# First block of a two-block model: lo parts of 15 weight tiles by an adding DMA, second gate moved behind the last chunk sum, two output tables moved ahead of the recurrence

## Chip, cores and metric

The kernel runs on one core of a Trainium2 chip. The metric is the device time of one execution in microseconds; several executions are taken and the median is given.

## What is computed

The reference takes x of 512 tokens by 1024 channels through two blocks. Only the first is touched by the change. It is, cut to what matters:

```python
h = _rms_norm(x, pre_norm_g)
z_q, z_kv, z_kr, g_attn, u_ssm, g_ssm = split(h @ w_in)       # 256, 128, 64, 512, 512, 512
attn = _mla_attention(z_q, z_kv, z_kr, ...)                   # 4 heads, q and k with a rotary part
attn = _rms_norm(attn) * silu(g_attn)
ssm = _s5_bidirectional(u_ssm, ...)                           # 32 groups, 64 complex states, both directions
ssm = gelu(ssm); ssm = ssm * sigmoid(ssm @ w_glu + b_glu)
ssm = _rms_norm(ssm) * silu(g_ssm)
x = x + _rms_norm(concat([attn, ssm]) @ w_out)
```

The second block is two layers of sparse and forgetting attention, each with a feed-forward part.

## The kernel before

**Precision by splitting.** A product of float32 matrices is made of three matmuls (`mm3`, lines 172 to 176). Each operand is split into hi, its value rounded to the matmul's format, and lo, what is left: hi times hi, hi times lo and lo times hi are added up in PSUM. For weights this is done in `weights` (lines 146 to 167): SyncE loads a block of 512 KB into a staging tile `wst` (two buffers), ScalarE casts it to hi (`whi`, line 143), VectorE subtracts, staging minus hi, to lo (`wlo`, line 144). With `pool` set, GpSimd makes lo instead; the diff leaves that branch alone. There are four `whi` and four `wlo` buffers, so a block's split can start only when an earlier block's matmuls are done with theirs.

**The first block in order.** `block1` (lines 305 to 844) norms and transposes x into `xT`, and multiplies it by the weights of u. The state-space part runs by chunks: for each of eight slices of four groups, `f_slice` (lines 463 to 481) makes a table on VectorE (`table`, lines 450 to 458: a product into `tb`, a product into `ot`, and their sum), transposes it on TensorE (`ftr`), copies it out on ScalarE (`f`) and multiplies it by u (`vps`, line 478), which gives the chunk sums; ScalarE copies them into `st`. The recurrence over the chunk sums (`recur`, lines 503 to 518) is a chain of VectorE operations on `st`: 13 steps of four operations (lines 498 to 501) and 16 fix-up operations (lines 517 and 518).

Next in program order are the two gates (lines 610 to 617, each four outputs of 24 matmuls by `feat`), the z tiles (`z_tile`, lines 629 to 653: `tok`, a norm with a row sum on GpSimd, a transpose), the matmuls for V (line 666), for the rotary part of q (lines 668 to 686, four rounds of matmul, VectorE, ScalarE, transpose), and then a list of rounds (line 770) which interleaves three kinds of generators: `prep(s)` (lines 533 to 562: the output table of slice s, its store to `Ed` in DRAM, and the kernel matrix `kps` with its store to `Kd`), `y_slice(s)` (lines 566 to 600: reads both back, copies `st` into `X`, and multiplies) and `head(h)` (lines 704 to 767: one attention head). After them come the gated unit, the output projection and the norms.

**What sets the order.** The program order gives priorities alone. A scheduler of the framework places each engine's instructions by priority and by a simulated timeline, so an engine can run a later stage's instruction while an earlier one's inputs are missing; once placed, the order on an engine is fixed and each instruction waits for its inputs. `tc.issue_after(ins)` adds an edge: the instructions traced inside it on the engine of `ins` stand behind `ins` in that engine's order. Tiles of one tag share a few buffers: `tb` two (tag E), `ot` and the fix-ups' `fx` one (tag et).

Of the kernel before, what the change touches and what calls it, by code (L numbers as in the profile page):

```python
# [12 lines left out]
AF = mybir.ActivationFunctionType  # L13
OP = mybir.AluOpType
# [13 lines left out]
SL0 = 3  # L28
# [12 lines left out]
def rounds(items, heads=()):  # L41


    items, r = list(items), 0
    while items:
        now = [x for x in items if x[0] <= r]
        late = [x for x in now if x[1] in heads]
        done = []
        for x in [x for x in now if x[1] not in heads] + late[1:] + late[:1]:
            if next(x[1], done) is done:  # L50
                done.append(x)
        items = [x for x in items if x not in done]
        r += 1
# [10 lines left out]
class Net:  # L64
# [78 lines left out]
        self.nc.scalar.copy(hi, src)  # L143
        self.nc.vector.tensor_tensor(lo, src, hi.bitcast(F32), OP.subtract)  # L144

    def weights(self, blocks, cw=512, n=2, pool=False, into=None, stage=None):

        nc = self.nc
        hs, ls = [], []
        for i, b in enumerate(blocks):  # L150
            if stage is None:
                st = self.wpool.tile([128, n, 1024 // n], F32, tag="stage", bufs=2, name="wst")
                nc.sync.dma_start(st[:, :, :cw], b)
            else:
                st = stage[:, i]
            h, l = into or (self.wpool.tile([128, n, 1024 // n], F32R, tag=t, bufs=self.slots["w"], name=t)
                            for t in ("whi", "wlo"))
            if pool is True or pool and i in pool:
                nc.scalar.copy(h[:, :, :cw], st[:, :, :cw])
                for j in range(n):  # L160
                    self.lo(l[:, j, :cw], st[:, j, :cw], h[:, j, :cw])
            else:
                self.split(h[:, :, :cw], l[:, :, :cw], st[:, :, :cw])
            for j in range(n):
                hs.append(h[:, j, :cw])
                ls.append(l[:, j, :cw])
        return hs, ls
# [137 lines left out]
    def block1(self):  # L305

        nc, A, tc = self.nc, self.A, self.tc
        mm = nc.tensor.matmul
# [46 lines left out]
        def feat(wh, wl, m):  # L355
            p = self.ps("mm")
            ms = slice(m * 128, (m + 1) * 128)
            for k in range(8):
                self.mm3(self.tiled(p), wh[k][:, ms], wl[k][:, ms], xh[k], xl[k], k == 0, k == 7)
            return p  # L360
# [99 lines left out]

        st = self.act(shape=[128, G, 2, 8, 8], name="st", tag="C")

        def f_slice(s):
            gs = slice(s * 4, s * 4 + 4)
            ft = table(FP, FQ, br[:, gs], bi[:, gs], s)
            yield
            f = []
            for r in range(2):
                p = self.ps("sc" if s % 2 else "tr", "ftr")
                for gg in range(4):  # L470
                    nc.tensor.transpose(p[:, gg * 128:(gg + 1) * 128], ft[:, gg, r], self.ident)
                f.append(self.act(shape=[128, 4, 128], name="f", tag="PT"))
                nc.scalar.copy(f[r].rearrange("p g e -> p (g e)"), p)
            yield
            pv = self.ps("o", "vps").rearrange("p (g r c) -> p g r c", r=2, g=4)
            for r in range(2):
                for gg in range(4):
                    mm(pv[:, gg, r], f[r][:, gg], U[:, s * 4 + gg], start=True, stop=True)
            for ps_, o in ((slice(0, 64), 1), (slice(64, 128), -1)):
                nc.scalar.copy(st[ps_, gs].rearrange("p g r j s -> p (g r) j s"),  # L480
                               pv[ps_, :, :, ::o].rearrange("p g r (s j) -> p (g r) j s", j=8))
# [84 lines left out]
        def y_slice(s):  # L566
# [21 lines left out]
            if s % 2 == 1:  # L588
# [10 lines left out]
                nc.scalar.activation(q, q, AF.Tanh, scale=math.sqrt(2.0 / math.pi))  # L599
                nc.vector.scalar_tensor_tensor(sg[:, m], q, 1.0, p, OP.add, OP.mult)  # L600

        recur()


# [3 lines left out]
        nc.vector.tensor_scalar(gn[:, 1], gn[:, 1], 0.125, None, OP.mult)  # L608
        gate = [self.b8([128, 4, 512], F32, name="gate") for _ in range(2)]
        for i in range(2):  # L610
            wh, wl = self.weights([A["w1_in"][1 + i, j] for j in range(4)])
            for m in range(4):
                p = feat(wh, wl, m)
                th = self.act(name="th", tag="c")
                nc.scalar.activation(th, p, AF.Tanh, scale=0.5)
                nc.scalar.activation(gate[i][:, m], p, AF.Copy, scale=gn[:, i, m:m + 1])
                nc.vector.scalar_tensor_tensor(gate[i][:, m], th, 1.0, gate[i][:, m], OP.add, OP.mult)
# [6 lines left out]
        gqk = self.act(shape=[128, 384], name="gqk", tag="PT")  # L624
        nc.sync.dma_start(gqk, A["gqk"].to_broadcast([128, 384]))
        Z = [self.b8([128, 4, 512], name=n) for n in ("zh", "zl")]
        wh, wl = self.weights([A["w1_z"][i] for i in range(4)], 448)

        def z_tile(t):
            ts = slice(t * 128, (t + 1) * 128)  # L630
# [24 lines left out]
        rounds((t, z_tile(t)) for t in range(NT))  # L655


        wqr_h, wqr_l = self.weights([A["w_uq_r"]], 256)
        wk_h, wk_l = self.weights([A["w_ukv_t"]])
        wq_h, wq_l = self.weights([A["w_uq_n"]])  # L660
        V = [self.b8([128, 4, 512], name=n) for n in ("vh", "vl")]
        QR = self.b8([128, 4, 512], name="QR")
        for t in range(NT):
# [40 lines left out]
        def head(h):  # L704
# [52 lines left out]
            if SPLIT:  # L757
# [9 lines left out]
            nc.vector.tensor_tensor(gate[0][:, h], o, gate[0][:, h], OP.mult)  # L767

        sg = self.b8([128, 4, 512], F32, name="sg")
        rounds([(s, prep(s)) for s in range(8)] + [(SL0 + s, y_slice(s)) for s in range(8)]  # L770
               + [(HEAD0[h], head(h)) for h in range(4)])


# [753 lines left out]
```

## Time and profile before

| | us |
|---|---|
| median of 3 runs | 1667.33 |
| lowest, highest | 1665.48, 1668.69 |
| the profiled execution | 1673.57 |
| its span | 1671.8 |
| TensorE busy | 1593.8 (95%) |
| VectorE busy | 951.2 (57%) |
| ScalarE busy | 794.3 (48%) |
| GpSimd busy | 402.4 (24%) |

The profile is of one execution. PE is TensorE, DVE is VectorE, ACT is ScalarE, POOL is GpSimd, SPq is SyncE's queue of DMA issues. Matmuls overlap in their records, so a busy TensorE is not one at its peak; its granted clock, at full speed 1.00, tells how fast it could go. The first block takes the first 345 us or so of the span.

### The profile page before, as it was taken

To read this page: it belongs to the slowest core of one execution; us is meant where nothing else is said; L and a number is where in the kernel's file an instruction comes from. 1 tells how busy PE (TensorE), PEld (TensorE's weight loads), DVE (VectorE), ACT (ScalarE), POOL (GpSimd) and SP (SyncE) were. 2 spreads that over 40 slices of the span, in tenths; PEclk is the share of its full clock that TensorE was granted. 3 is DMA by queue.
4 is the path that set the end of the run, shared out by engine and by line. 5 is a ranking of instruction groups with operands and counts; after the bars stand their busy time and mean duration, and the time that the engine had idled before them with its cause. 6 is when DMAs were issued, how large, how long until landed. Compare 5 with 4: busy or idle time off the path is not lost.

```text
span 1671.8 us, 22665 instructions
## 1 busy us (share of the span) xinstructions
PE 1593.8 (95%) x8240; PEld 1345.8 (80%) x8240; DVE 951.2 (57%) x1863; ACT 794.3 (48%) x1548; POOL 402.4 (24%) x492
## 2 busy tenths in 40 slices
PE   7996899999999999999999999999989999999998
PEld 6884687787888888888888888788868888888886
DVE  8978767754687865323333365478875532333334
ACT  6634476543677845333232444368774433323242
POOL 2000013313455712001010140345580210101012
PEclk9998899999999999999999999899999999999999
DMA  5211452544322442332333334512234133333332
GB/s 172 75 56 38 129 146 76 184 119 156 92 59 53 119 134 75 96 95 89 101 101 101 114 109 128 161 45 58 64 102 126 51 101 101 101 101 101 101 96 81
DMA packets 71407, 167.44 MB, mean 100 GB/s; under 512 B 14464, under 2 KB 23168, under 8 KB 71296
## 3 DMA queue, kind: packets, MB, share of 16 engines
q1 hardware_dynamic: 70528, 165.21, 32.3%
q8 instruction: 65, 1.06, 0.3%
q10 hardware_dynamic: 768, 0.79, 0.2%
q14 instruction: 46, 0.38, 0.1%
HBM read 145.80 MB, written 10.98 MB: 94 GB/s over the span
## 4 chain that ended last, share of the span: by engine, by line
PE 70%; DVE 7%; ACT 3%; issue 3%; DMA 2%; POOL 1%; ACTq 1%; DVEq 0%; POOLq 0%; SPq 0%
PE mm L176 19%; PE mm L174 19%; PE mm L175 19%; PE cps L983 2%; PE ptr L943 2%; DVE sc L918 1%; DVE pt L144 1%; PE sc L917 1%; PE sc L914 1%; PE oacc L952 1%; PE oacc L953 1%; DVE wlo L144 1%; ACT ysq L206 1%; DMA ql<-ql 1%; ACT sc L921 1%
## 5 line engine op out<-in xcount | busy, mean ns | idle before, releaser
L144 DVE TENSOR_TENSOR wlo<-wst,whi 128x1024 fp32r<-128x1024 f32 (+3 forms) x209 | 253.7, 1218 | 248.8 <-ACT whi L143 245.1
L174 PE MATMUL mm<-xT,whi 128*128 128x512 f32 (+1 forms) x896 | 337.8, 380 | 4.3 <-ACT kf L1083 2.8
L143 ACT CAST whi<-wst 128x1024 fp32r<-128x1024 f32 (+3 forms) x209 | 215.3, 1034 | 256.6 <-PE mm L176 123.7
L175 PE MATMUL mm<-xT,whi 128*128 128x512 f32 (+1 forms) x896 | 335.5, 376 | 0.0
L176 PE MATMUL mm<-xT,wlo 128*128 128x512 f32 (+1 forms) x896 | 326.3, 376 | 0.9 <-DVE wlo L144 0.8
L1367 POOL TENSOR_TENSOR relu<-relu 128x512 f32<-128x512 f32 x64 | 67.1, 1048 | 539.6 <-ACT relu L1366 539.6
L176 PE MATMUL mm<-whi,hl 128*128 128x512 f32 x512 | 195.9, 389 | 0.0
L175 PE MATMUL mm<-wlo,hh 128*128 128x512 f32 x512 | 195.9, 389 | 0.0
L174 PEld LDWEIGHTS mm<-xT,whi 128*128 128x128 f32 x896 | 168.2, 189 | 33.4 <-ACT kf L1083 3.6
L176 PEld LDWEIGHTS mm<-xT,wlo 128*128 128x128 f32 x896 | 168.7, 189 | 32.1 <-DVE wlo L144 1.8
L175 PEld LDWEIGHTS mm<-xT,whi 128*128 128x128 f32 x896 | 168.9, 189 | 27.4
L174 PE MATMUL mm<-whi,hh 128*128 128x512 f32 x512 | 188.2, 389 | 0.0
L921 ACT ACTIVATE sc<-sc,mn 128x512 f32<-128x512 f32 x192 | 107.1, 559 | 32.9 <-DVE mn L918 25.2
L144 DVE TENSOR_TENSOR hl<-relu,hh 128x512 fp32r<-128x512 f32 x64 | 51.8, 810 | 119.4 <-ACT hh L143 117.1
L144 DVE TENSOR_TENSOR pt<-ptr,pt 128x256 fp32r<-128x256 f32 (+1 forms) x160 | 95.7, 605 | 40.0 <-ACT pt L143 39.1
L176 PEld LDWEIGHTS mm<-whi,hl 128*128 128x128 f32 x512 | 96.1, 188 | 20.0
L175 PEld LDWEIGHTS mm<-wlo,hh 128*128 128x128 f32 x512 | 96.1, 188 | 19.9
L174 PEld LDWEIGHTS mm<-whi,hh 128*128 128x128 f32 x512 | 96.1, 188 | 19.9
L1366 ACT ACTIVATE relu<-mm 128x512 f32<-128x512 f32 x64 | 38.3, 598 | 148.3 <-PE mm L176 148.3
L918 DVE CUSTOM_DVE_ANT_0 sc<-sc,c_mask 128x512 f32<-128x512 f32 x192 | 87.3, 483 | 34.2 <-PE sc L917 30.9
L143 ACT CAST pt<-ptr 128x256 fp32r<-128x256 f32 (+1 forms) x160 | 81.5, 515 | 52.4 <-PE ptr L943 41.3
L930 POOL TENSOR_SCALAR sc<-sc,smx,gt 128x512 f32<-128x512 f32 (+3 forms) x128 | 78.9, 627 | 82.9 <-DVE smx L925 54.4
(394 smaller groups left out, 2961.5 us busy)
## 6 DMA issues: line engine op xcount, KB each, us to landing
wst<-in_w_up_t SPq DMA_DIRECT2D x64, 512.0 KB
wst<-in_w_down_t SPq DMA_DIRECT2D x64, 512.0 KB
wst<-in_w_in_m SPq DMA_DIRECT2D x24, 512.0 KB
wst<-in_w_in_a SPq DMA_DIRECT2D x16, 512.0 KB
x<-x SPq DMA_DIRECT2D x32, 256.0 KB
w<-in_cw SPq DMA_DIRECT2D x32, 256.0 KB
wst<-in_w_out_t SPq DMA_DIRECT2D x16, 512.0 KB
wst<-in_w_in SPq DMA_DIRECT2D x8, 512.0 KB
```

What stands on the lines that cost most here:

```text
L143: self.nc.scalar.copy(hi, src)
L144: self.nc.vector.tensor_tensor(lo, src, hi.bitcast(F32), OP.subtract)
L174: mm(ps, lh, rh, start=first, stop=False)
L175: mm(ps, lh, rl, start=False, stop=False)
L176: mm(ps, ll, rh, start=False, stop=last)
L918: nc.vector.tensor_tensor_reduce(out=sreg[i], in0=p, in1=self.mask[:, 512 - w:512], scale=1.0, scalar=3e38, op0=OP.add, op1=OP.min, accum_ ...
L921: self.mark = nc.scalar.activation(sreg[i], sreg[i], AF.Exp, bias=mn[:, i:i + 1], scale=-1.0, accum_out=sm[:, i:i + 1])
L930: nc.gpsimd.tensor_scalar(sreg[i], sreg[i], sm[:, i:i + 1], rgate[:, i:i + 1], OP.mult, OP.mult)
L943: self.pe = nc.tensor.transpose(p[:, c:c + 128], sreg[i][:, j * 128:(j + 1) * 128], self.ident)
L983: nc.tensor.matmul(p[:, :62], st[:, j], bk[:, jj].rearrange("p g n -> p (g n)"), start=jj == 0, stop=jj == 15)
L1366: nc.scalar.activation(a, p, AF.Relu)
L1367: nc.gpsimd.tensor_tensor(a, a, a, OP.mult)
```

## The change

`weights` gets an argument `add`. With it, ScalarE makes hi as before and also writes minus hi into the lo tile, and then GpSimd issues a DMA that adds the block from DRAM to what is in the lo tile, so lo becomes weight minus hi. It is used for the 15 tiles of the first block between the recurrence's tables and the heads: two gates (4 each), z (4), `w_uq_r`, `w_ukv_t` and `w_uq_n`. The second gate's matmuls are set behind the last `vps` on TensorE. The generators of `prep` are made ahead of the recurrence and the first two run to their first `yield`, that is, through loads of `cc`, table and store to `Ed`. In the rounds, `prep(s)` starts one round sooner from slice 1 on, and each `y_slice` one round sooner.

```diff
-    def weights(self, blocks, cw=512, n=2, pool=False, into=None, stage=None):
+    def weights(self, blocks, cw=512, n=2, pool=False, into=None, stage=None, add=False):
...
-            if pool is True or pool and i in pool:
+            if add:
+                nc.scalar.copy(h[:, :, :cw], st[:, :, :cw])
+                nc.scalar.activation(l[:, :, :cw], st[:, :, :cw], AF.Copy, scale=-1.0)
+                nc.gpsimd.dma_start(l[:, :, :cw], b, accum_op=OP.add)
+            elif pool is True or pool and i in pool:
...
+        last = [None]
+
         def f_slice(s):
...
-                    mm(pv[:, gg, r], f[r][:, gg], U[:, s * 4 + gg], start=True, stop=True)
+                    last[0] = mm(pv[:, gg, r], f[r][:, gg], U[:, s * 4 + gg], start=True, stop=True)
...
+        preps = [prep(s) for s in range(8)]
+        for g_ in preps[:2]:
+            next(g_)
         recur()
...
-            wh, wl = self.weights([A["w1_in"][1 + i, j] for j in range(4)])
+            wh, wl = self.weights([A["w1_in"][1 + i, j] for j in range(4)], add=True)
             for m in range(4):
-                p = feat(wh, wl, m)
+                with ExitStack() as late:
+                    if i:
+                        late.enter_context(tc.issue_after(last[0].ins))
+                    p = feat(wh, wl, m)
...
-        wh, wl = self.weights([A["w1_z"][i] for i in range(4)], 448)
+        wh, wl = self.weights([A["w1_z"][i] for i in range(4)], 448, add=True)
...
-        wqr_h, wqr_l = self.weights([A["w_uq_r"]], 256)
-        wk_h, wk_l = self.weights([A["w_ukv_t"]])
-        wq_h, wq_l = self.weights([A["w_uq_n"]])
+        wqr_h, wqr_l = self.weights([A["w_uq_r"]], 256, add=True)
+        wk_h, wk_l = self.weights([A["w_ukv_t"]], add=True)
+        wq_h, wq_l = self.weights([A["w_uq_n"]], add=True)
...
-        rounds([(s, prep(s)) for s in range(8)] + [(SL0 + s, y_slice(s)) for s in range(8)]
+        rounds([(max(0, s - 1), preps[s]) for s in range(8)] + [(SL0 - 1 + s, y_slice(s)) for s in range(8)]
                + [(HEAD0[h], head(h)) for h in range(4)])
```

## Rows read from the trace of the kernel before

**Rows 1.** The page: busy time, share of the span and instructions of each engine.

```profile
PE 1593.8 (95%) x8240; PEld 1345.8 (80%) x8240; DVE 951.2 (57%) x1863; ACT 794.3 (48%) x1548; POOL 402.4 (24%) x492
```

**Rows 2.** Stretches: from:to, length, busy of PE, PEld, DVE, ACT, POOL; clock, DMA share, GB/s.

```profile
44.50:107.00 62.50, 62.50 (x375) 54.97 (x374) 50.47 (x69) 35.94 (x60) 0.00 (x0) 1.00 0.18 52
...
97.00:209.00 112.00, 88.54 (x442) 71.44 (x442) 94.83 (x181) 45.51 (x95) 9.03 (x14) 0.88 0.26 78
...
209.00:345.00 136.00, 127.56 (x726) 106.00 (x725) 94.20 (x140) 87.25 (x150) 39.94 (x42) 0.98 0.43 137
...
154.00:167.00 13.00, 7.13 (x18) 4.88 (x18) 10.73 (x16) 6.80 (x9) 0.76 (x1) 0.61 0.01 1
167.00:186.00 19.00, 11.56 (x52) 9.39 (x53) 16.04 (x22) 4.60 (x12) 1.20 (x2) 0.76 0.42 139
...
97.00:154.00 57.00, 47.60 (x219) 38.70 (x218) 53.19 (x113) 20.10 (x44) 4.31 (x8) 0.94 0.18 58
```

**Rows 3.** Timeline of VectorE: start, us, engine, line, operation, tiles, count, idle before.

```profile
82.50 1.22 DVE L457 TENSOR_TENSOR tb<-tb,ot 128x1024 f32<-128x1024 f32 x1
...
97.23 0.69 DVE L498 TENSOR_TENSOR rt<-PA,st 128x512 f32<-128x512 f32 x1 [1.04 <-ACT st L480]
...
166.99 1.59 DVE L456 TENSOR_TENSOR ot<-EQ,cc 128x1024 f32<-128x1024 f32 x1
```

**Rows 4.** Timeline of TensorE: last transposes and last chunk sum.

```profile
87.97 1.04 PE L471 MATMUL ftr<-c_ident,tb 128*128 128x128 f32 x8
...
94.09 1.89 PE L478 MATMUL vps<-U,f 128*128 128x64 f32 x16
```

**Rows 5.** Stretch of the gate matmuls (tile mm) alone: busy PE, PEld, DVE, ACT.

```profile
76.40:94.30 17.90, 10.81 (x44) 8.04 (x44) 0.00 (x0) 1.73 (x4) 1.00 0.28 89
```

**Rows 6.** Timeline of ScalarE: casts of weights, copies to st and X, cast of qkh.

```profile
45.56 1.05 ACT L143 CAST whi<-wst 128x1024 fp32r<-128x1024 f32 x1
...
96.03 1.17 ACT L480 COPY st<-vps 64x512 f32<-64x512 f32 x2 [0.56 <-PE vps L478]
...
111.27 0.94 ACT L143 CAST whi<-wst 128x896 fp32r<-128x896 f32 x1 [1.12 <-DMA wst<-in_w_z]
...
128.71 1.05 ACT L143 CAST whi<-wst 128x1024 fp32r<-128x1024 f32 x1 [0.43 <-PE mm L176]
...
155.26 1.12 ACT L576 COPY X<-st 64x512 f32<-64x512 f32 x1 [1.70 <-DVE st L518]
...
159.77 0.58 ACT L143 CAST qkh<-mm 128x512 fp32r<-128x512 f32 x1
```

**Rows 7.** Timeline of TensorE: where lo is used, and first scores and kps.

```profile
52.84 1.91 PE L471 MATMUL ftr<-c_ident,tb 128*128 128x128 f32 x16
...
106.81 0.36 PE L174 MATMUL mm<-whi,xT 128*128 128x448 f32 x1
...
131.81 0.51 PE L175 MATMUL mm<-wlo,zh 128*128 128x512 f32 x1
...
160.41 0.80 PE L174 MATMUL sc<-qkh 128*128 128x512 f32 x1 [5.30 <-ACT qkh L143]
...
170.75 4.99 PE L549 MATMUL kps<-tb,bb 128*48 128x128 f32 x32 [2.53 <-DVE tb L457]
```

**Rows 8.** Groups of VectorE, 41.8 to 84 us: count, busy us, mean ns, idle.

```profile
L144 DVE TENSOR_TENSOR wlo<-wst,whi 128x1024 fp32r<-128x1024 f32 x6 | 7.3, 1221 | 0.0
```

**Rows 9.** Groups of VectorE, 97 to 167 us.

```profile
L517 DVE TENSOR_TENSOR fx<-st,PA 128x784 f32<-128x784 f32 x8 | 7.8, 974 | 0.1
L518 DVE TENSOR_TENSOR st<-st,fx 128x784 f32<-128x784 f32 x8 | 7.8, 972 | 0.0
L144 DVE TENSOR_TENSOR wlo<-wst,whi 128x896 fp32r<-128x896 f32 (+2 forms) x7 | 7.4, 1068 | 0.4 <-ACT whi L143 0.4
```

**Rows 10.** Timeline of GpSimd: its first operation behind 60 us.

```profile
116.55 0.22 POOL L183 TENSOR_SCALAR rs_t<-zss 128x2 f32<-128x2 f32 x1 [93.72 <-ACT zn L635]
```

**Rows 11.** Timeline of SyncE's queue: the last two loads of z weights.

```profile
105.70 1.54 SPq L153 DMA_DIRECT2D wst<-in_w_z  x2
```

## Prediction before the run

> **What bounds the kernel now.** I read the page's first part, then the table of stretches, then the timelines of single engines where TensorE falls idle. Over the whole span TensorE is busy 95% [rows 1], so only a stretch in which it is not full has anything to give. The diff touches the first block alone, and there the hole is between 97 and 209 us: 88.5 of 112 us busy at a mean granted clock of 0.88, against 127.6 of 136 us behind it, to 345 us [rows 2]. That leaves 23.5 us of idle time, which is the most that filling can bring, plus something from the clock. Its two worst parts are 154 to 186 us, 18.7 of 32 us busy at 0.61 and 0.76, where VectorE is busy 26.8 us: VectorE sets that stretch, not TensorE.
>
> Why does VectorE run late? The recurrence on `st` starts at 97.23 us and resumes the tables at 166.99 [rows 3]. Its start needs the last chunk sum (`vps`), and the timeline of TensorE shows that sum queued behind gate matmuls: the last table was ready at 83.7 us [rows 3], yet its transposes start at 87.97 and its `vps` at 94.09 [rows 4]. 44 matmuls of the gates, 10.8 us of TensorE, stand in that stretch [rows 5]; all but two (at 78.7 us) belong to the second gate.
>
> **The change part by part.**
>
> *Second gate behind the last chunk sum.* The work is the same, only its place changes. From the table's end at 83.7 us I add transposes 1.04 and `vps` 1.9 [rows 4], with copies of f and copies to `st` of 1.2 each [rows 6]: about 89 us, some 8 us before 97.23. TensorE loses its filler up to there and may idle a few us; what it still has is gate 0. Queued behind the added wait on TensorE are the second gate's 96 matmuls, and behind them the z tiles, which need the second gate's weight slots. As TensorE was full from 44.5 to 107 us [rows 2], no work is saved: the z tiles begin at 106.8 [rows 7] or a little after, not sooner.
>
> *Lo of 15 weight tiles.* VectorE loses 6 tiles between 44.5 and 84 us, 7.3 us [rows 8], two before that, and 7 behind 97 us, 7.4 us [rows 9]. So the recurrence, which shares VectorE with everything else, should end near 166.9 - 8 - 7.4 = 151.5 us, and nearer 145 if the tables in front of it gain too. ScalarE gains 15 scaled copies of the cast's kind, 0.94 to 1.05 us each [rows 6], about 14 us; it is under half busy from 97 to 154 us (20.1 of 57 us) [rows 2], so I cost them through the chain they lengthen alone. GpSimd's queue holds nothing between 22 and 116 us [rows 10]; later the z tiles' row sums can stand behind an adding DMA that waits for its minus hi, 1 to 2 us in the worst tile.
>
> The price is latency. Where VectorE made lo within 1.1 us after the cast, the new lo needs minus hi (0.95) and a transfer. No adding DMA is in this trace. The nearest row is the plain load of the same tile: two issues end at 107.24 us [rows 11] and the cast that waits for the second starts at 111.27 [rows 6], 4.0 us. An add has to read what it adds to, so I bound it by 4.0 and twice that, 8.0, and take 4.5, near the plain load, since the share of the DMA engines is only 0.18 from 97 to 154 us [rows 2]. Three places can wait for it. Gate 0, fourth tile: cast ends 46.6, minus hi 47.6, lands 51.6 at 4.0; TensorE has 36 gate matmuls and then transposes at 52.84 [rows 7], so nothing at 4.0 and 2.8 us at 8.0. The z tiles: the fourth cast ends 112.2, lo lands 117.2 instead of 113.3, so 3.9 us (7.9 at twice). The V matmuls: the cast of w_ukv ends 129.8 [rows 6], lo lands 134.8; TensorE used it at 131.81 [rows 7], so 3.0 us (7.0). Sum 7 us at 4.0, about 8 at 4.5, 17.7 at 8.0.
>
> The page "DMA: Bandwidth & Descriptors" of the Trainium skill (Anatomy of one DMA) fits a GpSimd-issued transfer as 2.0 us plus bytes over 436 GB/s; an estimate by it for 512 KB is 3.2 us, and the sum of the waits would fall to about 4.6 us. No run here shows such a transfer, and the measured plain load is slower than that.
>
> *What the earlier recurrence gives back.* First, the first scores: they wait 5.3 us for `qkh` until 160.41 [rows 7]; that cast (159.77) stands on ScalarE behind the four copies to `X`, the first of which was held until 155.26 by the recurrence's `st` [rows 6]. With the recurrence done by 151 those copies go out earlier: -5.3. Second, the four rounds of the rotary part of q, which interleave on VectorE with the 16 fix-up operations, 15.6 us in all [rows 9]: I take -6, a bit under half. So the first scores come at 160.4 + 8 - 5.3 - 6 = 157, about 3.5 us earlier.
>
> *Two output tables ahead of the recurrence.* Their first product already runs early; the second product and the sum, 4 operations, 5.3 us of VectorE from 166.99 on [rows 3], move into VectorE's idle time before the recurrence. What waits for them is `kps`, 2.53 us idle and then 4.99 us at the low clock [rows 7], in the stretch where TensorE has least. It can move into the new waits for lo. I take -6.5. Moved with them are the two stores to `Ed` and two loads of `cc` on SP's queue; there they stand between the z weights, whose loads wait for a stage buffer anyhow, so nothing. In the rounds, `prep` and `y_slice` come one round sooner against the heads; both end in the same work, no cost.
>
> Sum: -3.5 - 6.5 = -10 us. From 209 us on TensorE is nearly full (127.6 of 136 us) [rows 2], so what is gained by then is kept and no new gain arises. The profiled execution is 1673.6 us, its span 1671.8; the median of the runs is 1667.3, 6.2 below. The sum against the profiled one is 1663.6, against the median **1657**.
>
> **The rivals.**
>
> *The adding DMA is slow.* If one lands 8 us after its issue, the waits are 17.7 us and cancel the gains (17.8); from there on every us costs about 3. At 10 us: 6 us slower, 1673. For it: three places wait on it within 90 us, and TensorE, when idle, falls to half its clock (0.61 in 154 to 167 us). Against it: DMA engines little used. Chance 0.2.
>
> The Trainium skill, "SBUF — State Buffer" (SBUF: two separate sides), has a rule that ends here too: GpSimd cannot write descriptors while VectorE runs a two-port operation such as an fp32 copy. By it, the adding DMAs would start only between such operations. VectorE is full here, but the same page says that two-input operations have no two-port mode, and the operations that fill it here are of that kind [rows 3, 8, 9]; so I give it no more than a part of that 0.2.
>
> *TensorE's order sets the stretch.* z cannot start before 107 us, and if the waits for lo (8 us) take all that the recurrence gives except the tables' share, minus what the scheduler's new order loses, the result is -2 us, 1665. For it: the 62.5 us of full TensorE up to 107 us are untouched. Chance 0.15.
>
> *VectorE's whole relief arrives.* 14.7 us of lo, 8 us of earlier start and 5.3 us of tables are 28 us off VectorE; if the tables of the later slices also move ahead, 154 to 186 us shrinks by its idle 13.3 us, and with 3 us of clock and the -3.5 above this is -20, 1647. Chance 0.17.
>
> **How the numbers follow.** My forecast, -4 to -15 us, has 0.48. Faster by over 0.2% (3.3 us, about what a measurement here can tell from no change): forecast and full relief, 0.65. Same: 0.15. Slower: 0.20. The range, 1646 to 1672, reaches from full relief to an adding DMA of just under 10 us.
>
> **What would show it.** In the changed profile: the first `rt` near 85 to 90 us instead of 97.23; no `wlo` on VectorE before 137 us; the first z matmul at 107 to 110; waits of the V matmuls on a DMA into `wlo`; first scores near 157, `kps` of slices 0 and 1 before them; and the stretch 209 to 345 us shifted as a whole. I am wrong if the landing of an adding DMA is over 8 us, if the recurrence starts no earlier, or if the first scores come later than 160 us.

## The result and the profile after

The changed kernel takes 1687.3 us in the median of 4 runs (1685.3 to 1692.5), beside 1666.4 us for the kernel before; the ratio is 1.0129, with a 95% interval of 1.0107 to 1.0152. It is 21 us slower, where 10 us faster was forecast and the range ended at 1672. The profiled execution took 1685.25 us, its span 1683.4.

First the page: the busy line of the engines, as in [rows 1], and the two DMA queues with packets, MB and the share of the 16 DMA engines' time. Queue q0 holds the adding DMAs; the kernel before has none.

```profile
PE 1589.8 (94%) x8240; PEld 1340.0 (80%) x8240; DVE 937.2 (56%) x1848; ACT 807.6 (48%) x1563; POOL 417.1 (25%) x507
...
q1 hardware_dynamic: 70528, 165.21, 32.2%
q0 software_dynamic: 2800, 7.34, 2.4%
```

VectorE lost 15 instructions and 14.0 us of work (951.2 before), ScalarE gained 15 and 13.3 us: both as the prediction counted them. TensorE does the same 8240 matmuls. The loss is in where they stand. The stretches of [rows 2] again, for the changed kernel:

```profile
44.50:107.00 62.50, 59.54 (x385) 51.08 (x386) 49.23 (x67) 39.92 (x66) 4.27 (x5) 0.97 0.49 123
97.00:209.00 112.00, 85.70 (x399) 68.74 (x398) 74.74 (x150) 48.59 (x94) 15.98 (x20) 0.86 0.46 111
209.00:345.00 136.00, 124.51 (x725) 104.50 (x724) 83.06 (x135) 82.38 (x137) 30.86 (x30) 0.96 0.40 123
154.00:167.00 13.00, 8.38 (x44) 7.09 (x43) 10.02 (x19) 11.74 (x20) 4.45 (x6) 0.90 0.42 84
167.00:186.00 19.00, 11.53 (x46) 9.15 (x47) 14.35 (x24) 4.77 (x10) 0.90 (x1) 0.68 0.54 158
97.00:154.00 57.00, 43.07 (x175) 33.73 (x174) 36.90 (x79) 17.91 (x35) 6.99 (x9) 0.88 0.57 129
```

From 97 to 154 us VectorE is busy 36.9 instead of 53.2 of 57 us, and TensorE 43.1 instead of 47.6. Of VectorE's 16.3 us only a part is work that is gone (7.4 us of lo between 97 and 167 us [rows 9]); the rest is waiting and work that now comes later, and TensorE does less too. The share of the DMA engines there rose from 0.18 to 0.57. The mean granted clock of TensorE is lower in one stretch (0.68 instead of 0.76 from 167 to 186 us) and higher in another (0.90 instead of 0.61 from 154 to 167 us); over 97 to 209 us it is 0.86 beside 0.88, so by these means the clock has little part in the loss.

What TensorE waits for is in its timeline (start, us, line, tiles, and in brackets the idle time before and what ended it): four of its first uses of a lo, then the first scores.

```profile
45.40 0.80 PE L181 MATMUL mm<-xT,wlo 128*128 128x512 f32 x1 [4.53 <-DMA wlo<-in_w_in]
...
114.44 0.80 PE L181 MATMUL mm<-xT,wlo 128*128 128x512 f32 x1 [6.11 <-DMA wlo<-in_w_in]
...
136.38 0.74 PE L180 MATMUL mm<-wlo,xT 128*128 128x448 f32 x1 [4.64 <-DMA wlo<-in_w_z]
...
170.70 0.80 PE L180 MATMUL mm<-wlo,zh 128*128 128x512 f32 x1 [6.72 <-DMA wlo<-in_w_ukv_t]
...
191.97 0.71 PE L179 MATMUL sc<-qkh 128*128 128x512 f32 x2
```

Against [rows 7]: V's lo is used at 170.7 instead of 131.8 us, the first scores come at 192.0 instead of 160.4. The view of the tile `wlo` between 30 and 200 us sums the waits of TensorE's matmuls for lo (24.6 us in two lines, in eight places) and gives the time from issue to landing. L181 uses the lo of the two gates, L180 those of z and V:

```profile
  PE mm L181: 12.6, 5
  PE mm L180: 12.0, 3
...
DMA to landing us min/median/max: 5.7/7.8/10.4
```

The chain that ended last, between 100 and 200 us (start, us, what), runs through these landings one after another, and through a plain load of z's weights that itself took 7.66 us:

```profile
107.42 6.97 DMA wlo<-in_w_in
...
129.25 7.66 DMA wst<-in_w_z
...
139.01 7.47 DMA wlo<-in_w_z
...
162.69 7.97 DMA wlo<-in_w_ukv_t
```

Each set of weights needs the slots of the set before it. Its casts begin when that set's matmuls end, and those wait for a landing. So in this chain a landing is paid once for each set, in series.

Last, VectorE: the start of the recurrence and its last operation, in the changed kernel (the first two lines) and the last operation before, where the start is at 97.23 [rows 3]:

```profile
92.55 0.69 DVE L505 TENSOR_TENSOR rt<-PA,st 128x512 f32<-128x512 f32 x1 [3.04 <-ACT st L487]
...
166.64 0.96 DVE L525 TENSOR_TENSOR st<-st,fx 128x784 f32<-128x784 f32 x1
...
165.98 0.97 DVE L518 TENSOR_TENSOR st<-st,fx 128x784 f32<-128x784 f32 x1
```

It begins 4.7 us sooner and ends 0.7 us later, though its engine is rid of all 15 lo, 7 of them (7.4 us) in this very stretch [rows 9]. The waits of VectorE between 92 and 167 us (line, releaser, us in total, times, longest) say why:

```profile
DVE zn L652 <- POOL rs_r L190: 8.0, 2, 7.4
DVE k L565 <- ACT k L561: 6.9, 1, 6.9
DVE rt L505 <- ACT st L487: 3.0, 1, 3.0
DVE gate L631 <- ACT gate L630: 2.4, 4, 1.1
DVE tb L461 <- issue: 2.3, 1, 2.3
DVE zl L144 <- ACT zh L143: 2.2, 1, 2.2
```

VectorE's order is fixed, and between the operations of the recurrence stand the gates' products, the z tiles' norms and `k` of the early tables. Each of them waits for TensorE, TensorE waits for a lo, and the recurrence stands behind. The same view of the kernel before, from 97 to 167 us, sums to 5.7 us in six lines.

### The profile page after: what moved, and what is told of

It reads as the page before. It is cut to its first block, busy times and chain, and to the rows that moved or that the text cites. A ratio compares the mean times of both kernels' runs of the same rounds, so it can differ in the third digit from the quotient of the medians.

```text
span 1683.4 us, 22711 instructions
## 1 busy us (share of the span) xinstructions
PE 1589.8 (94%) x8240; PEld 1340.0 (80%) x8240; DVE 937.2 (56%) x1848; ACT 807.6 (48%) x1563; POOL 417.1 (25%) x507
## 3 DMA queue, kind: packets, MB, share of 16 engines
q1 hardware_dynamic: 70528, 165.21, 32.2%
q0 software_dynamic: 2800, 7.34, 2.4%
## 4 chain that ended last, share of the span: by engine, by line
PE 69%; DVE 9%; issue 8%; ACT 6%; DMA 4%; POOL 2%; SPq 1%; ACTq 0%; DVEq 0%; POOLq 0%
PE mm L179 20%; PE mm L181 20%; PE mm L180 19%; PE ptr L957 2%; DVE sc L932 1%; PE cps L997 1%; DVE pt L144 1%; ACT sc L935 1%; PE sc L931 1%; DVE wlo L144 1%; PE oacc L966 1%; PE sc L928 1%; PE oacc L967 1%; ACT ysq L211 1%; DMA swap<-raw 1%
## 5 line engine op out<-in xcount | busy, mean ns | idle before, releaser
L144 DVE TENSOR_TENSOR wlo<-wst,whi 128x1024 fp32r<-128x1024 f32 (+1 forms) x194 | 235.4, 1217 | 252.2 <-ACT whi L143 248.5
L181 PE MATMUL mm<-xT,wlo 128*128 128x512 f32 (+1 forms) x896 | 328.2, 379 | 13.5 <-DMA wlo<-in_w_in 12.6
L180 PE MATMUL mm<-xT,whi 128*128 128x512 f32 (+1 forms) x896 | 336.7, 377 | 0.0
L143 ACT CAST whi<-wst 128x1024 fp32r<-128x1024 f32 (+1 forms) x194 | 200.1, 1035 | 250.8 <-PE mm L181 123.4
L181 PEld LDWEIGHTS mm<-xT,wlo 128*128 128x128 f32 x896 | 169.4, 189 | 46.9 <-DMA wlo<-in_w_in 14.9
L179 PEld LDWEIGHTS mm<-xT,whi 128*128 128x128 f32 x896 | 168.7, 189 | 34.5 <-ACT kf L1097 3.6
L180 PE MATMUL mm<-wlo,hh 128*128 128x512 f32 x512 | 196.0, 389 | 0.0
L181 PE MATMUL mm<-whi,hl 128*128 128x512 f32 x512 | 196.0, 389 | 0.0
L180 PEld LDWEIGHTS mm<-xT,whi 128*128 128x128 f32 x896 | 169.5, 190 | 27.6
L144 DVE TENSOR_TENSOR pt<-ptr,pt 128x256 fp32r<-128x256 f32 (+1 forms) x160 | 95.5, 604 | 41.0 <-ACT pt L143 40.2
L181 PEld LDWEIGHTS mm<-whi,hl 128*128 128x128 f32 x512 | 96.1, 188 | 19.9
L180 PEld LDWEIGHTS mm<-wlo,hh 128*128 128x128 f32 x512 | 96.1, 188 | 19.9
```

Of the source, the lines that this page charges most:

```text
L179: mm(ps, lh, rh, start=first, stop=False)
L180: mm(ps, lh, rl, start=False, stop=False)
L181: mm(ps, ll, rh, start=False, stop=last)
```

## The experiments

Seventeen kernels are set side by side here, the two of this case among them. The time is the ratio to the runs of the kernel before on the same chip, and that ratio less one times 1666 us. The other columns are from one profiled execution of each kernel, in us (for the moved gate alone it took 1671.5 us, 14 more than the median, and its first block shows none of that): the start of the recurrence (`rt`) and of its last operation, the first scores, and the first and last matmul of the tile `nps`, the sums of squares for the norms of the attention and state-space outputs. All work up to the output projection is ahead of those.

| kernel | recurrence | first scores | nps | ratio (95%) | us |
|---|---|---|---|---|---|
| before | 97.2 to 166.0 | 160.4 | 279.5 to 302.9 | 1 | 0 |
| after | 92.5 to 166.6 | 192.0 | 294.9 to 324.2 | 1.0129 (1.0107 to 1.0152) | +21.5 |
| adding DMAs alone | 96.6 to 163.8 | 192.1 | 294.1 to 317.5 | 1.0093 (1.007 to 1.0116) | +15.5 |
| gate and tables alone | 90.1 to 154.5 | 167.3 | 271.6 to 295.0 | 0.998 (0.9965 to 0.9994) | -3.3 |
| after, plain load | 87.6 to 149.5 | 173.6 | 279.7 to 309.3 | 1.0029 (1.0016 to 1.0042) | +4.8 |
| gate alone | 90.6 to 153.4 | 168.7 | 272.9 to 296.3 | 0.9962 (0.9943 to 0.9981) | -6.3 |
| tables alone | 97.4 to 170.4 | 162.4 | 279.8 to 303.3 | 1.0 (0.9981 to 1.0018) | 0 |
| adds in gate 0 | 96.3 to 161.7 | 172.6 | 276.8 to 300.2 | 0.9978 (0.9955 to 1.0001) | -3.7 |
| adds in z | 98.0 to 166.1 | 167.9 | 280.2 to 303.6 | 1.0011 (0.9994 to 1.0028) | +1.8 |
| adds in q and V | 98.6 to 168.6 | 166.3 | 281.0 to 304.4 | 1.0023 (1.0006 to 1.0041) | +3.8 |
| adds in the second gate | 91.7 to 158.6 | 160.3 | 273.5 to 296.8 | 0.9979 (0.9964 to 0.9995) | -3.5 |
| gate moved, adds in z | 90.5 to 154.1 | 178.3 | 278.5 to 301.9 | 1.0017 (1.0001 to 1.0034) | +2.8 |
| gate moved, adds in second gate | 92.4 to 158.7 | 167.5 | 272.0 to 295.4 | 0.9954 (0.9938 to 0.9971) | -7.7 |
| after without gate 0's adds | 94.8 to 164.2 | 182.8 | 288.6 to 312.1 | 1.0065 (1.0046 to 1.0083) | +10.8 |
| after without tables | 96.0 to 160.8 | 189.7 | 290.1 to 313.5 | 1.0049 (1.0033 to 1.0066) | +8.2 |
| gate moved, lo of gates on GpSimd | 95.5 to 161.7 | 170.4 | 276.1 to 299.5 | 0.9996 (0.9979 to 1.0012) | -0.7 |
| the same, z's lo too | 95.6 to 162.5 | 182.9 | 284.1 to 307.5 | 1.0034 (1.0018 to 1.005) | +5.7 |

The shift of the last `nps` from 302.9 follows the measured time within 5 us in every row, so the difference is made ahead of it, as far as rows of one execution can tell; the code behind it is the same in all.

### The parts one by one

**The adding DMAs alone**, everything else as before:

```diff
-            wh, wl = self.weights([A["w1_in"][1 + i, j] for j in range(4)])
+            wh, wl = self.weights([A["w1_in"][1 + i, j] for j in range(4)], add=True)
...
-        wh, wl = self.weights([A["w1_z"][i] for i in range(4)], 448)
+        wh, wl = self.weights([A["w1_z"][i] for i in range(4)], 448, add=True)
...
```

`w_uq_r`, `w_ukv_t` and `w_uq_n` get `add=True` likewise.

> The kernel before with the adding DMAs for all 15 tiles, and nothing moved. Theory A (the late landing of the adding DMA is the loss: 5.7 to 10.4 us from issue to landing in the changed kernel, and 24.6 us of TensorE waits on lo): nearly the whole loss stands here too, 1682 to 1695 us. Rival B (the moved second gate and the tables cause it, because the second gate's weights come late): 1664 to 1672 us. Under A TensorE waits on a DMA into lo at gate 0, at z and at V for 15 us or more in sum.

Measured: 1679.6 us, +15.5 us, a little under the 1682 of theory A and far above B; landings of 5.3 to 9.7 us with a median of 7.6. The first scores come at the same 192 us as in the changed kernel. The adds by themselves account for most of the loss.

**Gate and tables alone**: the changed kernel with `add=True` taken out of all five calls.

> The changed kernel with lo made on VectorE as before: only the second gate and the two tables moved. Theory A: no loss, and the gain that the prediction gave to the order, so 1655 to 1664 us, with the recurrence's first operation 5 to 9 us ahead of 97.23 and the first scores ahead of 160.4. Rival B: 1675 us or more.

Measured: -3.3 us. The recurrence starts at 90.1 and ends at 154.5 us, as theory A had it. But the first scores, which were to come sooner, come 7 us later than before, and the kernel is still faster: in the kernel before they cannot be what sets the end.

**The changed kernel with a plain load in place of the add**, so that the DMA overwrites minus hi:

```diff
-                nc.gpsimd.dma_start(l[:, :, :cw], b, accum_op=OP.add)
+                nc.gpsimd.dma_start(l[:, :, :cw], b)
```

> The changed kernel with the same transfer from GpSimd's queue, but without the add (lo then holds the whole weight, so the output leaves out the subtraction). If the add itself is slow (it reads its destination and works element by element), landings fall from a median of 7.8 us to 3.5 to 4.5 us and the time to 1660 to 1672. If GpSimd's issuing (software descriptors, cast to the matmul's format) is what is slow, landings stay at 6.5 us or more and the time at 1680 or more.

Measured: +4.8 us, 1670.4, inside the range for a slow add. Its landing in the view of the tile `wlo`, a little above the 3.5 to 4.5 us expected:

```profile
DMA to landing us min/median/max: 3.8/4.9/9.9
```

and its queue on the page, with the same packets and bytes as above:

```profile
q0 software_dynamic: 2800, 7.34, 1.4%
```

So the add, not the way through GpSimd's queue, makes 2.9 us of the landing and 16.7 of the 21.5 us (by the two intervals, give or take some 4). TensorE's waits for lo, 24.6 us in the changed kernel, are 10.9 us here, 3.5 of them in the gates. And a landing near the 4.5 us that the prediction took still does not make the kernel faster.

**The moved gate alone** (`issue_after` and `last`, nothing else) and **the tables alone** (`preps`, the two `next`, and the rounds one sooner):

> The kernel before with the second gate behind the last chunk sum and nothing else. Prediction's step: the recurrence starts 5 to 9 us sooner and the first scores follow it, 1659 to 1664 us. Rival: TensorE up to the z tiles is the bound, the second gate's end does not move, and the time is that of before within 3 us; or the gate's end moves back by the time that TensorE idles before the last chunk sum, and it is slower.

> The kernel before with the two output tables ahead of the recurrence and the rounds one sooner, and nothing else. The moved gate alone gave 1657.1 and gate and tables together 1660.7. If the parts add up, this one is 1667 to 1672, a loss of 1 to 5 us; if the tables are a gain by themselves that is lost beside the moved gate, 1657 to 1664.

Measured: -6.3 us and 0. The moved gate is the part that gains; at 1657.1 us it is 2 us below its range, and its first scores did not follow the recurrence but come 8 us later. The tables alone do nothing that can be measured: the interval is 3 us to either side.

### One set of weights at a time

In each, one set of the kernel before gets the adding DMA, by `add=i == 0`, by `add=True` at z, at the three of q and V, and by `add=i == 1`.

> The kernel before with the adding DMA in the first gate's four tiles alone. Theory A with TensorE's order: the gate's first matmuls stand ahead of the transposes of u on TensorE, so a wait of 4 to 5 us for lo stops the state-space chain too: u's transposes end 6 to 9 us later and the time is 1669 to 1676. Rival (the first gate is filler with slack, so a late lo costs nothing): within 3 us of before.

> The kernel before with the adding DMA in the four z tiles alone. Theory A (each set of weights waits its own landing, since its buffers come free only when the set before is used up): a landing near 8 us in place of 1.1 on VectorE, so z's TensorE work ends 5 to 8 us later and the time is 1669 to 1675. Rival (a lateness here is hidden, as VectorE sets 107 to 167 us): within 3 us of before.

> The kernel before with the adding DMA in w_uq_r, w_ukv_t and w_uq_n alone. Theory A: the V matmuls wait for one landing, 4 to 7 us, behind z; 1667 to 1673. Rival: the wait is hidden behind VectorE's recurrence, and VectorE, 3 tiles lighter, gives some back; 1662 to 1667.

> The kernel before, with the lo of the second gate's four weight tiles alone made by minus hi plus the adding DMA; the order of the work is unchanged. Theory (two branches, the later one sets the end): this set's landings push the first scores back by 5 to 8 us, from 160.4 to 165-168, and since the recurrence branch still binds, with its end at 164-168 us, the time stays within 3 us of before (1662-1668 us). The lateness of the first scores of the single sets then sums to near the 32 us that all fifteen show. Rival (every wait of TensorE for a landing is paid): slower than before by the 5 to 8 us, 1671 us or more.

The first scores move by +12.2, +7.5, +5.9 and -0.1 us, 25.5 in sum beside 31.7 for the adds alone, but the time moves by -3.7, +1.8, +3.8 and -3.5 us, the first two inside their intervals. None costs what it delays. Theory A, by which a late set is paid for, failed in gate 0 (1660.6 us, where it had 1669 or more) and in z (1666.7, where it had 1669 or more); q and V came out at the border of its range (1667.2). In the second gate the first scores were to come 5 to 8 us late and the time was to stay; they are not late, and the time is 3 us under its range. The landings of these single sets have medians of 7.8, 8.2, 7.4 and 7.7 us, so an add takes as long with three or four of them as with fifteen.

Gate 0 was the place that the prediction costed at nothing. In the kernel before, ScalarE's cast of its first tile, and TensorE's first use of a lo and its transposes of u (the first three lines); then TensorE with adds in gate 0 alone:

```profile
35.67 1.06 ACT L143 CAST whi<-wst 128x1024 fp32r<-128x1024 f32 x1 [0.18 <-PE mm L176]
...
40.00 0.39 PE L176 MATMUL mm<-xT,wlo 128*128 128x512 f32 x1
...
42.36 2.23 PE L379 MATMUL utr<-c_ident,yt 64*128 64x64 f32 x32
...
45.23 0.79 PE L181 MATMUL mm<-xT,wlo 128*128 128x512 f32 x1 [4.47 <-DMA wlo<-in_w_in]
...
49.04 0.80 PE L181 MATMUL mm<-xT,wlo 128*128 128x512 f32 x1 [0.88 <-DMA wlo<-in_w_in]
...
51.05 3.67 PE L384 MATMUL utr<-c_ident,yt 64*128 64x64 f32 x32
```

In the kernel before, gate 0's lo is first used at 40.00 and the 32 transposes `utr` start at 42.36 and take 2.23 us. With the adds the first gate matmul that needs a lo, still ahead of them in TensorE's order, waits 4.5 us for it, and they come 8.7 us later. What follows the idle stretch also ran longer: the 32 transposes took 3.67 us, and over 25 to 60 us of this kernel the granted clock is 0.80 instead of 1.00.

The second gate's adds are free by contrast: TensorE waits 0.4 us for them in all, since there its minus hi are written at 68 to 81 us and TensorE has other work until they land, and VectorE is rid of them ahead of the recurrence (91.7 instead of 97.2 us). In the changed kernel TensorE waits up to 6.1 us for the same set, and its hi are cast at 86 to 105 us. Gate 0 holds its slots: without gate 0's adds (below) the adding DMAs of the second gate are issued at 70.1 to 83.3 us again, and TensorE waits for none of them.

### Two branches

Two things must be done before the heads and the state-space outputs are: the first scores, and the recurrence. From the rows of the first eight experiments I read that the first `nps` comes 102 to 106 us behind the first scores or 109 to 114 us behind the recurrence's last operation, whichever is later. In the kernel before the recurrence is later by some 14 us (166 + 112 = 278 against 160.4 + 104 = 264). So it has room for late scores, and the single sets cost little. A kernel that ends the recurrence sooner has no such room. The test is the adds in z, once more, behind the moved gate:

```diff
+                with ExitStack() as late:
+                    if i:
+                        late.enter_context(tc.issue_after(last[0].ins))
+                    p = feat(wh, wl, m)
...
+        wh, wl = self.weights([A["w1_z"][i] for i in range(4)], 448, add=True)
```

> The second gate behind the last chunk sum, as in the run of the moved gate alone, and z's four weight tiles with the adding DMA; nothing else is changed. Theory (two branches): the adding DMA on z pushed the first scores back by 7.5 us in the order of before and cost 1.8 us there, since the recurrence branch was bound; with the gate moved, the first scores (168.7 us there) bind, so the same edit now moves them to 174-177 us and costs nearly its whole lateness: 1662-1667 us, 5 to 9 us above the moved gate alone. Rival (effects of the parts simply add): 1.8 us above the moved gate alone, 1657-1660 us.

Measured: ratio 1.0017, beside 0.9962 for the moved gate alone: 0.55%, 9.2 us (give or take some 4), just above the 5 to 9 expected; effects that simply add would have made it 1.8. In the profiled executions the last `nps` moves by 5.6 us, and by 0.7 in the order of before. The recurrence ends at the same time (154.1 and 153.4), the scores move from 168.7 to 178.3, a little more than expected. The same edit costs 2 us on one branch and 9 on the other.

Over all the rows the later of (scores + 104) and (recurrence + 112) is within 4 us of the first `nps`, seven kernels made after the constants were read among them. The constants are read off and not derived: which wait joins the branches was not traced.

### What was open: the tables inside the whole

The adds alone (+15.5) and the moved gate alone (-6.3) sum to +9; the whole is +21.5, though the tables alone are 0. Three more kernels: the changed one without the tables, the changed one without gate 0's adds, and the moved gate with adds in the second gate only.

> The changed kernel with the two output tables where they were before; all fifteen adding DMAs and the moved gate stay. Theory: the first scores stay near 192 us (188-195) and the first nps matmul at 292-298 us, but ScalarE has two hi casts instead of four ahead of the aoh casts, so the last nps matmul follows 23.4 us behind the first and not 29.3: 1678-1683 us, some 6 us below the changed kernel. Rival (the 6 us are contention or the clock, which the adding DMAs bring): 29 us between the nps matmuls and 1685 us or more.

> The changed kernel with gate 0's four lo made by VectorE's subtraction again; the other eleven adding DMAs, the moved gate and the tables stay. Theory (two branches): the first scores, at 192.0 us in the changed kernel, come 8 to 14 us sooner, at 178-184 us, the recurrence's end stays off the path, the first nps matmul comes at 282-288 us, the stretch to the last one shrinks from 29.3 to 23.4 us since two hi casts instead of four stand ahead of the aoh casts, and the time is 1666-1675 us. Rival (the landings of the later sets alone set the first scores): they stay at 188 us or more and the time at 1679 us or more.

> The second gate behind the last chunk sum and the adding DMA for that gate's four weight tiles alone; the other lo are VectorE's. Theory: alone in the old order this set left the first scores at 160.3 us and moved the recurrence's end from 166.0 to 158.6 us; behind the moved gate the first scores (168.7 us with the moved gate alone) bind and VectorE's relief gives nothing more: within 4 us of the moved gate alone, 1653-1661 us. Rival: the moved gate's matmuls now wait for the landings ahead of the z stage, the first scores come 5 us or more later and the time is 1662 us or more.

Without the tables: +8.2 us, what the two parts sum to. So beside the adds the tables cost 13 us (1.0129 against 1.0049), more than the 6 expected. Two places show part of it. One is the stretch from the first to the last `nps`, 29.3 us with the tables and 23.4 without. ScalarE's timeline in the changed kernel:

```profile
295.09 1.07 ACT L143 CAST whi<-wst 128x1024 fp32r<-128x1024 f32 x1
296.05 0.62 ACT L143 CAST sfh<-gf 128x512 fp32r<-128x512 f32 x1
296.56 0.69 ACT L802 ACTIVATE gth<-mm,bg 128x512 f32<-128x512 f32 x1
297.14 1.05 ACT L143 CAST whi<-wst 128x1024 fp32r<-128x1024 f32 x1
298.08 4.01 ACT L143 CAST aoh<-gate 128x512 fp32r<-128x512 f32 x4
```

and without the tables:

```profile
287.69 1.06 ACT L143 CAST whi<-wst 128x1024 fp32r<-128x1024 f32 x1
288.63 0.70 ACT L799 ACTIVATE gth<-mm,bg 128x512 f32<-128x512 f32 x1
289.21 4.32 ACT L143 CAST aoh<-gate 128x512 fp32r<-128x512 f32 x4
293.24 1.15 ACT L143 CAST whi<-wst 128x1024 fp32r<-128x1024 f32 x1
```

The last weights of the block have four hi casts. In the changed kernel all four stand ahead of `aoh` on ScalarE, without the tables only two, and TensorE waits 3.41 us for `aoh` at 299.28. Of the kernels in the table only the changed one and its plain-load form have that order, and only they have the longer stretch (29.3 and 29.6; all others 23.4). The scheduler places those casts anew with each edit, far from where it was made.

The other place is SyncE's queue. With the tables, two stores to `Ed` (512 KB each) stand among the loads of the second gate's weights; here, from the timelines of SyncE's queue and of ScalarE, the two stores, the last of these loads and the cast that needs it:

```profile
87.02 0.33 SPq L547 DMA_DIRECT2D Ed<-tb  x1
...
89.66 0.38 SPq L547 DMA_DIRECT2D Ed<-tb  x1
90.13 0.90 SPq L154 DMA_DIRECT2D wst<-in_w_in  x1
...
105.11 1.05 ACT L160 CAST whi<-wst 128x1024 fp32r<-128x1024 f32 x1 [7.13 <-DMA wst<-in_w_in]
```

From the end of its issue, 91.03, that is 14.1 us for a plain load of 512 KB; one of 448 KB takes 4.0 in the kernel before [rows 6, 11]. Without the tables the two loads are issued by 93.89, and the cast that needs the second starts 7.4 us later:

```profile
91.67 2.22 SPq L154 DMA_DIRECT2D wst<-in_w_in  x2
...
101.28 1.06 ACT L160 CAST whi<-wst 128x1024 fp32r<-128x1024 f32 x1 [2.09 <-DMA wst<-in_w_in]
```

The first `nps` is 4.8 us sooner there. 5.9 and 4.8 us are 10.7 of the 13; the rest is within the intervals. That the late load makes all of the 4.8 us is not shown: the first scores are only 2.3 us sooner.

The plain-load form has the same stores in that queue and no adds. There the same load takes 10.0 us from the end of its issue to its cast:

```profile
85.23 0.92 SPq L154 DMA_DIRECT2D wst<-in_w_in  x1
...
96.17 1.05 ACT L160 CAST whi<-wst 128x1024 fp32r<-128x1024 f32 x1 [0.27 <-DMA wst<-in_w_in]
```

So the stores ahead of it in the queue count as well as the adds: 7.4 us with adds and no stores, 10.0 with stores and plain transfers, 14.1 with stores and adds.

Without gate 0's adds: +10.8 us, so they are worth 11 of the 21.5. First scores at 182.8 as expected, `nps` stretch 23.4, the time 3 us above what was expected. With adds in the second gate only, behind the moved gate: -7.7 us, and the moved gate alone -6.3; the difference is inside their intervals, as expected. These two are the best kernels of the study, 0.4% to 0.5% faster than before.

### Lo on GpSimd instead

If latency is the price, GpSimd could subtract without a DMA (`pool=True` for the two gates behind the moved gate, and then for z too).

> The second gate behind the last chunk sum, and the lo of both gates' eight weight tiles made by GpSimd's subtraction in place of VectorE's: no DMA is added and no landing is waited for. Theory: VectorE loses 8 subtractions of 7.3 us from the stretch before 110 us, so the recurrence ends sooner, and the lo come without a DMA; what binds is the first scores, at 168.7 us with the moved gate alone: 1650-1660 us if GpSimd's subtractions keep up with the casts. Rival: one subtraction takes GpSimd 9 us or more for a tile, gate 0's matmuls wait for it ahead of the recurrence's transposes, the first scores go beyond 172 us and the time is 1661 us or more.

> As the kernel with the lo of both gates made by GpSimd behind the moved gate, and the lo of z's four weight tiles by GpSimd as well. Theory: VectorE loses four more subtractions of some 6.4 us ahead of the z stage, the recurrence ends 3 to 8 us sooner than in that kernel, and with z's lo not behind the recurrence on VectorE the first scores come no later: 1647-1660 us. Rival: GpSimd falls behind in z (four tiles in a row), the first scores come 5 us or more later than in that kernel and the time is above it by as much.

Measured: -0.7 and +5.7 us, the rivals' times, though in the first the scores are not late (170.4); the recurrence is (161.7 instead of 153.4). The groups of GpSimd, 30 to 160 us (count, busy us, mean ns, idle and its releaser):

```profile
L875 POOL TENSOR_TENSOR wlo<-wst,whi 128x512 fp32r<-128x512 f32 x16 | 24.4, 1554 | 47.8 <-ACT whi L164 47.8
```

A half tile takes 1.55 us, a tile 3.1, beside VectorE's 1.22 [rows 8]. That is much shorter than the landing of an add, and the 9 us or more of the rival did not come true, but the recurrence starts at 95.5 us and not at 90.6, and with z also on GpSimd the scores come at 182.9 us. The timelines show why VectorE gains nothing. The first two lines are from this kernel, the third is the same operation with the moved gate alone:

```profile
78.09 4.08 POOL L875 TENSOR_TENSOR wlo<-wst,whi 128x512 fp32r<-128x512 f32 x2 [24.73 <-ACT whi L164]
78.86 2.17 DVE L461 TENSOR_TENSOR ot<-FQ,bbar 128x1024 f32<-128x1024 f32 x1
...
79.60 1.22 DVE L461 TENSOR_TENSOR ot<-FQ,bbar 128x1024 f32<-128x1024 f32 x1
```

While GpSimd subtracts, VectorE's two-input operations take some 1.0 us longer. From 36 to 95 us, over the operations that both kernels have, that is 11.7 us, and the eight lo that VectorE no longer makes are 9.8. How much of the later start follows from this was not measured by a run of its own.

## Why the prediction was wrong, point by point

**The work that moves: right.** 15 instructions off VectorE, 15 onto ScalarE, 14.0 and 13.3 us.

**The moved gate: right for the recurrence.** Moved alone, it lets the recurrence start at 90.6 us (forecast about 89) and end at 153.4, with the 15 lo still on VectorE. It is worth 6.3 us, though not by way of sooner first scores, which is how the sum had it.

**The price of a landing: wrong.** I took 4.5 us, by the plain load on SyncE's queue, within 4.0 to 8.0. Measured are 7.8 in the median, at the upper bound, and up to 10.4, beyond it. The low share of the DMA engines in the kernel before, 0.18, was the wrong thing to lean on: with adds in one set alone the landings are as long. The Trainium skill's fit for such a transfer ("DMA: Bandwidth & Descriptors", Anatomy of one DMA) gave an estimate of 3.2 us; the plain one measures 4.9 and the adding one 7.8, so the measurement decides against it here. (By the sum's own two places, z and V, the waits at 3.2 us would be 5.3 us and not the 4.6 written there.)

**Where it is waited for: wrong, and this weighs more.** The sum had three places and, per us of landing, 2.8 us of waits (8 at 4.5, 17.7 at 8.0). From the plain load (4.9) to the add (7.8) the time rises by 16.7 us, 5.8 per us, the slower plain loads beside the adds included. For z and V the terms hold: at 7.8 us they give 14.5 us, and TensorE waits 12.0. In the gates it waits 12.6 us, where the terms give 2.6. The step "gate 0: nothing" failed on the tile and on TensorE's order: I took the fourth tile and the transposes `ftr` at 52.84, but the first tile's lo is used at 40.0, its cast ends at 36.7 and its minus hi would end near 37.7, so that even a landing of 4.0 us comes late (measured: first use at 45.4), and the transposes `utr` at 42.4 stand behind it. The second gate was not listed; it waits 6.1 us once gate 0 is late. And the waits are in series: each set's casts wait for slots which the set before frees only after its own landing.

**What the earlier recurrence gives back: wrong.** By my own slope a landing of 4.9 us makes 9.1 us of waits and leaves -8.7; with that landing 10.9 us of waits are measured, not far off, and +4.8: the gains did not come. In the changed kernel the waits are 24.6 instead of 8 us, which in the sum's own terms is 16.6 of the 31 us between forecast and result; the rest is gain that did not come and what the tables cost. Of its terms, 6.5 us for the tables are 0 alone and a loss of 13 beside the adds. The copies to `X` and the rounds of q (-11.3) were booked as sooner first scores; but in the kernel before the recurrence is the later branch, by some 14 us, and the moved gate gains while its first scores come 8 us later. In the changed kernel, where the scores are the later branch, they come at 192.0 us instead of 157, over the 160 that I had named as a sign of being wrong. VectorE's relief became waits of VectorE, as its table of waits shows.

**"So nothing" for SyncE's queue: wrong.** I costed the moved stores to `Ed` at nothing because z's loads wait for a buffer anyhow. What stood behind them were the second gate's loads, one of which took 14 us.

**The rivals.** The first one, a slow adding DMA, was the right one, but its size was not: at 8 us it was to cancel the gains, and measured at 7.8 is a loss of 21.5. The lower clock that was named for it is hardly seen (0.86 beside 0.88 from 97 to 209 us). TensorE's order, the second, held in that z's first matmul comes at 112.2 us with the moved gate alone, not sooner than before; the time fell by 6.3 us all the same, not by 2.

## What to carry to other kernels

A latency put in front of many tiles in series is not paid where one looks for it, but at the first instruction of an in-order queue that needs it and for all that stands behind; list for each set of tiles what follows its first use on that engine, and who frees its slots. When two branches meet, an edit's price depends on which of them is late: a set of adds that cost 2 us alone cost 9 behind another edit that removed the slack. An edit that shows nothing alone can still cost beside another, so a change of several parts is measured by leaving one out as well as by putting one in.

## What the runs showed of the hardware

An adding DMA of 512 KB from DRAM into SBUF lands 7.8 us after its issue in the median, the same transfer without the add 4.9, with the same 2800 packets and 7.34 MB for fifteen. It also takes more of the DMA engines: 2.4% of 16 engines over 1683.4 us for 7.34 MB is 88 engine-us per MB, the plain one 51 (1.4% of 1669.0 us), and the loads on q1 52 (32.2% for 165.21 MB). GpSimd's issue of one took 0.84 to 1.12 us in the timeline, the plain one 0.54 to 0.79. A plain load on SyncE's queue, 4.0 us for 448 KB in the kernel before, took for 512 KB 7.4 us beside the adds, 10.0 with the tables' stores ahead of it in its queue and plain transfers on GpSimd's, and 14.1 with stores and adds. Beside a subtraction of GpSimd, VectorE's two-input operations took some 1.0 us longer (2.17 instead of 1.22 us). No run here tests the Trainium skill's rule on GpSimd's descriptors ("SBUF — State Buffer", SBUF: two separate sides) by itself.
